# Moving the activation blocks and split weights of a 17,544-matmul chain by multiples of 64 bytes, and four raw weight buffers instead of five

## Chip, cores and metric

The kernel runs on one core of a Trainium2 chip. The metric is the device time in microseconds, the median of three runs.

## The reference, cut to what matters

A first block (rms norm, three groups of dilated attention and a state space model in parallel, gates, an output product, a SwiGLU with 2816 hidden features) is applied to a sequence x of 256 tokens with 1024 features. Two layers of a second block follow, each a SwiGLU, an attention mix and another SwiGLU, on x and on a context of 256 tokens, with modulation vectors silu(c) @ w_mod + b_mod. All is float32. The products with weight matrices are what matters here:

```python
def swiglu(xn, w_ffn_in, w_ffn_out):
    gate, up = jnp.split(xn @ w_ffn_in, 2, axis=-1)
    return (jax.nn.silu(gate) * up) @ w_ffn_out
```

## The kernel before

**Products.** Activations stand feature-major: a block is 128 features (partitions) by 256 tokens, 1,024 bytes a partition. A product works through weight slabs of 128 x 1024 numbers (4,096 bytes a partition): eight blocks k of 128 x 128 weights, one for each block of activations. Both factors are split into two float32r parts, a high one and the rest, and each block takes three matmuls of 256 columns (`mm3_k`, lines 128 to 130): high weights on high activations, high weights on low activations, low weights on high activations. Each of the three has a weight load of its own in front. A slab on one stream (x or the context c) is so 24 matmuls.

**Weights.** `load_raw` (line 102) loads a slab on SP's queue into a buffer of the pool `raw` (five). `split_w` makes the high part on ScalarE (line 109, tile `wh`) and the rest on VectorE (line 110, tile `wl`), in pools of five buffers each. A `wh` or `wl` buffer comes free when TensorE has used it for all streams; a raw buffer when both splits have read it. `run` prepares a slab up to two units of work ahead, and in the products with two streams the second one follows the first by a distance. The framework's planner orders each engine's queue and picks the buffers from its own estimate of when they come free, so a raw buffer is not always the one used longest ago.

**Background.** The modulation vectors are made on VectorE: a piece loads a slab of w_mod into a raw buffer and multiplies it with silu(c) of one or two streams (line 938, tile `junk`), adding along the row. 144 pieces are spread between the units of the products by `weave`: 16 in the SwiGLU of the first block, up to 40 in each of the first three SwiGLUs of the second block. A SwiGLU is 68 units (22 gate, 22 up, 24 down); pieces stand between the seventh unit and the ninth from the end.

**Activations.** `new_act` gives a stream the tiles `ah` and `al` (high and low part), eight blocks each, one block directly behind the other. The hidden features of a SwiGLU are tiles of one block each (`hh`, `hl`), from pools of 14. The last part of the state space model is `ynh`, `ynl`; the attention's output in the first block `aoh`, `aol`.

**Places.** The compiled program lays the tiles of a pool one behind the other in a partition's memory. The start bytes of the operands of lines 128 to 130, and what is left over after division by 128:

| tiles | first start byte | pitch, bytes | remainder mod 128 |
|---|---|---|---|
| wh (5 buffers), and each 512-byte block in them | 42,176 | 4,096 | 64 |
| wl (5 buffers) | 62,656 | 4,096 | 64 |
| ah, al of x | 106,560 and 114,752 | 1,024 a block | 64 |
| ah, al of c | 131,136 and 139,328 | 1,024 a block | 64 |
| hh, hl (all) | 147,520 and 161,856 | 1,024 | 64 |
| ynh, ynl | 197,504 and 201,600 | 1,024 a block | 0 |
| aoh, aol | 152,096 and 156,192 | 1,024 a block | 32 |

One unit of the first block, the step size of the state space model (`w_dt`), has 32 weight columns a block instead of 128, so its weight load reads 128 bytes a partition instead of 512; its activations are `ah`, `al` of x.

Of the kernel before, what the change touches and what calls it, by code (L numbers as in the profile page):

```python
# [44 lines left out]
class Unit:  # L45
    """n weight slabs of src from index `at`, and what is done with them for each stream."""
# [5 lines left out]
def weave(units, steps, start=0, stop=0):  # L52
    """The steps spread evenly between the units, from the unit start on, up to stop units before the end."""
# [10 lines left out]
class Builder:  # L64
    def __init__(self, ctx, tc, A):
# [3 lines left out]
        self.raw_p = self.pool(ctx, "raw", 5)  # L69
# [8 lines left out]
        self.X, self.ACT, self.acc, self.bg, self.deferred = {}, {}, {}, [], []  # L78

# [19 lines left out]
    # ---------------------------------------------------------------- weights  # L99
# [5 lines left out]
    def split_w(self, raw, f):  # L105
        nc = self.nc
        h = self.w_p.tile([128, 1024], F32R, name="wh")
        lo = self.w_p.tile([128, 1024], F32R, name="wl")
        nc.scalar.copy(h[:, :f], raw[:, :f])  # L109
        nc.vector.tensor_tensor(lo[:, :f], raw[:, :f], h[:, :f].bitcast(F32), op=ALU.subtract)  # L110
        return h, lo
# [5 lines left out]
    def mm3(self, out, w, acts, m=128, first=True, last=True):  # L117
        """out[m, t] += sum over k of w[k, m] * act[k, t], each factor as the sum of two float32r parts."""
# [17 lines left out]
    def stream(self, s, src):  # L136
        """A stream of tokens, feature-major: the residual and what goes into the next product."""
# [5 lines left out]
    def new_act(self, s, n=KB):  # L143
        h = self.act_p[s].tile([128, n, T], F32R, name="ah" + s, tag="ah")
        lo = self.act_p[s].tile([128, n, T], F32R, name="al" + s, tag="al")
        return h, lo
# [4 lines left out]
    def lin(self, src, i, acts, evac, m=128, streams=None):  # L151
        """A unit of work: the product of slab i of src with acts(stream), feature-major, to evac(stream, psum)."""
        return Unit(src, i, 1, None, streams, (acts, m, evac))

    def later(self, f, key=None):
        """f is issued behind the next unit of work: TensorE does not wait for what f needs."""
        self.deferred.append((key, f))

    def step(self):
        """What was put off so far."""  # L160
# [4 lines left out]
    def flush(self, keys=None):  # L165
        """What was put off, or only what belongs to the keys, is issued now."""
# [8 lines left out]
    def run(self, items, streams, done=None, ko=0, ahead=2):  # L175
        """Units in order; the second stream follows the first at a distance, so that the end of one hides
        behind the other. The first ko units go k-outer in the last stream, while its activations are being made.
        Items that are no units are just called."""
# [76 lines left out]
    def background(self, n=1):  # L255
        """The next n pieces of the modulation vectors."""
# [6 lines left out]
    # ------------------------------------------------------------------ norms  # L263
# [10 lines left out]
    def rstd_cols(self, p, n, scale, eps, newton=False):  # L274
        """1 / sqrt(p * scale + eps) of [128, n] sums of squares, a token to a partition."""
# [6 lines left out]
        if newton:  # L282
            # one step on 1 / sqrt(v): r * (1.5 - 0.5 * v * r * r)
# [7 lines left out]
    def sums(self, key):  # L291
        """The sums of squares with a token to a partition."""
# [6 lines left out]
    def on_all(self, r):  # L299
        """A column for each 128 tokens -> the same row on every partition, in PSUM."""  # L300
# [6 lines left out]
    def rstd_all(self, key, width, eps=1e-6):  # L307
        """1 / sqrt(mean of squares + eps) of each token, on every partition (in PSUM)."""
        return self.on_all(self.rstd_cols(self.sums(key), 2, 1.0 / width, eps))

    def norm(self, s, src, scale, shift, h, lo, r):
        """(src * scale) * r + shift of each block, as float32r parts."""
# [10 lines left out]
    def norm_stream(self, s, scale, shift, final=None):  # L323
        """The normed and modulated stream, for the next products; behind the next two units of work.
        final: the gain of a norm of the residual itself that comes first (the sums of its squares: s + "f")."""
# [37 lines left out]
    # -------------------------------------------------------------------- ffn  # L363
    def ffn(self, wg, wu, wds, streams, gate, hid_p, steps, done, after=None):
# [28 lines left out]
        # what a product down needs is ready some units before it  # L393
# [1445 lines left out]
```

## Time and profile before

| | |
|---|---|
| runs | 2560.78, 2562.79, 2567.07 us; median 2562.79 us |
| profiled execution, span from the first to the last instruction | 2558.6 us |
| TensorE busy | 2486.2 us, 97% of the span |
| VectorE busy | 1656.2 us, 65% |
| ScalarE busy | 1082.6 us, 42% |
| mean granted clock of TensorE | 0.985 |

The profiled execution's own time is not listed apart from its span; the span is 4.2 us under the median of the runs. Matmuls overlap in the records (each is shown as some 0.28 us long), so the busy share of TensorE doesn't tell how fast it goes: the distance from one start to the next does.

### The profile page before, as it was taken

To read this page: it belongs to the slowest core of one execution; us is meant where nothing else is said; L and a number is where in the kernel's file an instruction comes from. 1 tells how busy PE (TensorE), PEld (TensorE's weight loads), DVE (VectorE), ACT (ScalarE), POOL (GpSimd) and SP (SyncE) were. 2 spreads that over 40 slices of the span, in tenths; PEclk is the share of its full clock that TensorE was granted. 3 is DMA by queue.
4 is the path that set the end of the run, shared out by engine and by line. 5 is a ranking of instruction groups with operands and counts; after the bars stand their busy time and mean duration, and the time that the engine had idled before them with its cause. 6 is when DMAs were issued, how large, how long until landed. Compare 5 with 4: busy or idle time off the path is not lost.

```text
span 2558.6 us, 48101 instructions
## 1 busy us (share of the span) xinstructions
PE 2486.2 (97%) x19910; PEld 2359.6 (92%) x19910; DVE 1656.2 (65%) x3135; ACT 1082.6 (42%) x2057; POOL 15.7 (1%) x20
## 2 busy tenths in 40 slices
PE   6999999999999999999999999999999987999999
PEld 6999899999999999996599999999999987866999
DVE  4667787787766665768766666566454464667554
ACT  4557565535522322536743222243222243555443
POOL 0000000000000000000000000000000000000000
PEclk9999899999999999999999999999999998999999
DMA  7444455676444443331025444425455433332553
GB/s 225 148 155 160 133 165 188 209 246 202 153 160 159 161 154 120 122 113 59 1 71 167 157 158 158 143 98 165 149 167 163 135 92 80 105 95 81 173 181 124
DMA packets 117242, 364.28 MB, mean 142 GB/s; under 512 B 21050, under 2 KB 28730, under 8 KB 117024
## 3 DMA queue, kind: packets, MB, share of 16 engines
q1 hardware_dynamic: 114512, 355.73, 42.7%
q0 software_dynamic: 1008, 3.09, 1.0%
q8 instruction: 156, 2.56, 0.4%
q10 hardware_dynamic: 1504, 2.40, 0.3%
q14 instruction: 62, 0.51, 0.1%
HBM read 357.34 MB, written 3.82 MB: 141 GB/s over the span
## 4 chain that ended last, share of the span: by engine, by line
PE 59%; DMA 8%; DVE 5%; issue 2%; ACT 1%; DVEq 0%; ACTq 0%; SPq 0%
PE pm L128 17%; PE pm L129 16%; PE pm L130 16%; DMA wraw<-w_mod 7%; DVE junk L938 3%; DVE wl L110 2%; PE pt L1077 1%; DMA sin<-mla_sin 1%; PE pa L984 1%; PE pt L1008 1%; PE pa L1524 1%; PE pm L1276 1%; PE pm L1216 1%; PE pa L1292 0%; PE pm L1532 0%
## 5 line engine op out<-in xcount | busy, mean ns | idle before, releaser
L128 PE MATMUL pm<-ahx,wh 128*128 128x256 f32 x2936 | 841.7, 289 | 17.6 <-ACT q L483 8.0
L109 ACT CAST wh<-wraw 128x1024 fp32r<-128x1024 f32 (+4 forms) x535 | 539.9, 1012 | 707.1 <-PE pm L129 440.0
L129 PE MATMUL pm<-alx,wh 128*128 128x256 f32 x2936 | 834.9, 285 | 0.1
L130 PE MATMUL pm<-ahx,wl 128*128 128x256 f32 x2936 | 834.8, 285 | 0.0
L110 DVE TENSOR_TENSOR wl<-wraw,wh 128x1024 fp32r<-128x1024 f32 (+4 forms) x535 | 627.8, 1176 | 206.7 <-ACT wh L109 205.2
L128 PEld LDWEIGHTS pm<-ahx,wh 128*128 128x128 f32 x2936 | 558.3, 191 | 28.4 <-ACT q L483 8.2
L129 PEld LDWEIGHTS pm<-alx,wh 128*128 128x128 f32 x2936 | 560.5, 191 | 4.5 <-issue 2.7
L130 PEld LDWEIGHTS pm<-ahx,wl 128*128 128x128 f32 x2936 | 559.5, 191 | 2.7 <-issue 2.0
L128 PE MATMUL pm<-ahc,wh 128*128 128x256 f32 x1280 | 361.7, 284 | 4.4 <-ACT ahc L320 4.4
L130 PE MATMUL pm<-ahc,wl 128*128 128x256 f32 x1280 | 360.8, 282 | 0.0
L129 PE MATMUL pm<-alc,wh 128*128 128x256 f32 x1280 | 360.3, 282 | 0.0
L938 DVE SCALAR_TENSOR_TENSOR junk<-wraw,cactc 128x1024 f32<-128x1024 f32 x112 | 137.1, 1224 | 237.9 <-DMA wraw<-w_mod 237.9
L938 DVE SCALAR_TENSOR_TENSOR junk<-wraw,cactx 128x1024 f32<-128x1024 f32 x144 | 175.8, 1221 | 118.6 <-DMA wraw<-w_mod 117.6
L128 PE MATMUL pm<-hhx,wh 128*128 128x256 f32 x880 | 248.9, 283 | 0.0
L130 PE MATMUL pm<-hhx,wl 128*128 128x256 f32 x880 | 248.2, 282 | 0.0
L129 PE MATMUL pm<-hlx,wh 128*128 128x256 f32 x880 | 247.7, 281 | 0.0
L128 PEld LDWEIGHTS pm<-ahc,wh 128*128 128x128 f32 x1280 | 240.7, 189 | 6.8 <-ACT ahc L320 5.0
L130 PEld LDWEIGHTS pm<-ahc,wl 128*128 128x128 f32 x1280 | 241.5, 189 | 0.3
L129 PEld LDWEIGHTS pm<-alc,wh 128*128 128x128 f32 x1280 | 241.2, 189 | 0.6 <-DVE alc L321 0.2
L128 PEld LDWEIGHTS pm<-hhx,wh 128*128 128x128 f32 x880 | 165.9, 188 | 0.2 <-DVE xx L401 0.2
L129 PEld LDWEIGHTS pm<-hlx,wh 128*128 128x128 f32 x880 | 166.0, 189 | 0.0
L130 PEld LDWEIGHTS pm<-hhx,wl 128*128 128x128 f32 x880 | 165.6, 188 | 0.0
(465 smaller groups left out, 3339.2 us busy)
## 6 DMA issues: line engine op xcount, KB each, us to landing
wraw<-w_mod SPq DMA_DIRECT2D x144, 512.0 KB, 4.3
wraw<-f1g SPq DMA_DIRECT2D x44, 512.0 KB, 3.5
wraw<-f1u SPq DMA_DIRECT2D x44, 512.0 KB, 3.5
wraw<-f2g SPq DMA_DIRECT2D x44, 512.0 KB, 3.5
wraw<-f2u SPq DMA_DIRECT2D x44, 512.0 KB, 3.6
wraw<-f1d SPq DMA_DIRECT2D x32, 512.0 KB, 3.9
wraw<-f2d SPq DMA_DIRECT2D x32, 512.0 KB, 3.5
wraw<-w_xbc SPq DMA_DIRECT2D x24, 512.0 KB, 3.5
```

The costliest lines, as they stand in the source:

```text
L109: nc.scalar.copy(h[:, :f], raw[:, :f])
L110: nc.vector.tensor_tensor(lo[:, :f], raw[:, :f], h[:, :f].bitcast(F32), op=ALU.subtract)
L128: nc.tensor.matmul(out, h[:, c], ah, start=first, stop=False)
L129: nc.tensor.matmul(out, h[:, c], al, start=False, stop=False)
L130: nc.tensor.matmul(out, lo[:, c], ah, start=False, stop=last)
L938: nc.vector.scalar_tensor_tensor(junk, raw, 1.0, K.cact[s], op0=ALU.mult, op1=ALU.mult, accum_out=K.mcol[layer, s][:, j:j + 1])
L984: nc.tensor.matmul(self.p[:, c:c + nh], sq[self.rows, j * 128:(j + 1) * 128], self.sums, start=True, stop=True)
L1008: nc.tensor.matmul(r, self.sel[:, cs], self.r, start=True, stop=True)
L1077: nc.tensor.transpose(p[:, j * 128:(j + 1) * 128], b, K.ident)
L1216: nc.tensor.matmul(p[:, :nk], qa[s][rows, 2 * half + b, t * 128:(t + 1) * 128], ka[rows, k0:k0 + nk], start=True, stop=True)
L1276: nc.tensor.matmul(p[:, :nk], qb[s][rows, hd, t * 128:(t + 1) * 128], kb[rows, hd, k0:k0 + nk], start=True, stop=True)
L1524: nc.tensor.matmul(po[64 * e:64 * e + 64, :T], v[:, i, b * 128 + e * 64:b * 128 + e * 64 + 64], pts[i][:, e * 256:e * 256 + 256], start=i ...
```

## The change

The two parts of the activations get blocks of 272 numbers of which 256 are used, so a block starts 1,088 bytes behind the one before. The buffers of the split weights are 1,072 numbers long, and a slab stands 0, 64, 128 or 192 bytes behind the start of its buffer: the high part by the number of the split modulo 4, the low part by a quarter of that number modulo 4. Raw weights get four buffers. Comments and docstrings are dropped without a change in line numbers up to the constructor; one line is added there (`self.n_split`), and two in `split_w`.

```diff
-        self.raw_p = self.pool(ctx, "raw", 5)
+        self.raw_p = self.pool(ctx, "raw", 4)
...
+        self.n_split = 0
...
     def split_w(self, raw, f):
         nc = self.nc
-        h = self.w_p.tile([128, 1024], F32R, name="wh")
-        lo = self.w_p.tile([128, 1024], F32R, name="wl")
+        self.n_split += 1
+        place = lambda t, i: t[:, 16 * (i % 4):16 * (i % 4) + 1024]
+        h = place(self.w_p.tile([128, 1072], F32R, name="wh"), self.n_split)
+        lo = place(self.w_p.tile([128, 1072], F32R, name="wl"), self.n_split // 4)
...
     def new_act(self, s, n=KB):
-        h = self.act_p[s].tile([128, n, T], F32R, name="ah" + s, tag="ah")
-        lo = self.act_p[s].tile([128, n, T], F32R, name="al" + s, tag="al")
-        return h, lo
+        h = self.act_p[s].tile([128, n, T + 16], F32R, name="ah" + s, tag="ah")
+        lo = self.act_p[s].tile([128, n, T + 16], F32R, name="al" + s, tag="al")
+        return h[:, :, :T], lo[:, :, :T]
```

## Rows read from the trace of the kernel before

**Rows 1.** The page: span, busy time and instructions of each engine.
```profile
span 2558.6 us, 48101 instructions
...
PE 2486.2 (97%) x19910; PEld 2359.6 (92%) x19910; DVE 1656.2 (65%) x3135; ACT 1082.6 (42%) x2057; POOL 15.7 (1%) x20
```

**Rows 2.** Four SwiGLUs by stretch: span, busy us (instructions) of each engine, clock, DMA.
```profile
475.00:640.00 165.00, 164.71 (x1378) 163.98 (x1377) 128.25 (x197) 78.86 (x115) 0.00 (x0) 1.00 0.67 225
...
1345.00:1640.00 295.00, 294.73 (x2484) 294.52 (x2482) 189.28 (x323) 77.87 (x127) 0.00 (x0) 1.00 0.49 158
```

**Rows 3.** TensorE's groups by line: count, busy us, mean ns.
```profile
L128 PE MATMUL pm<-ahx,wh 128*128 128x256 f32 x2936 | 841.7, 289 | 17.6 <-ACT q L483 8.0 <-ACT ahx L320 6.2 <-ACT ahx L114 2.0
...
L128 PE MATMUL pm<-ahc,wh 128*128 128x256 f32 x1280 | 361.7, 284 | 4.4 <-ACT ahc L320 4.4
...
L128 PE MATMUL pm<-hhx,wh 128*128 128x256 f32 x880 | 248.9, 283 | 0.0
...
L128 PE MATMUL pm<-hhc,wh 128*128 128x256 f32 x528 | 148.7, 282 | 0.0
```

**Rows 4.** Timeline of TensorE, last SwiGLU, one stream: start us, length.
```profile
2500.02 0.28 PE L128 MATMUL pm<-hhx,wh 128*128 128x256 f32 x1
...
2504.34 0.28 PE L128 MATMUL pm<-ahx,wh 128*128 128x256 f32 x1
```

**Rows 5.** Timeline of TensorE, a SwiGLU with two streams.
```profile
1450.07 0.28 PE L128 MATMUL pm<-hhx,wh 128*128 128x256 f32 x1
...
1455.05 0.28 PE L128 MATMUL pm<-hhx,wh 128*128 128x256 f32 x1
```

**Rows 6.** Timeline of TensorE, three units with ynh, and an entry from aoh.
```profile
402.17 0.28 PE L128 MATMUL pm<-ynh,wh 128*128 128x256 f32 x1
...
404.64 0.28 PE L128 MATMUL pm<-ynh,wh 128*128 128x256 f32 x1
...
406.79 0.28 PE L130 MATMUL pm<-ynh,wl 128*128 128x256 f32 x1
...
410.19 0.28 PE L130 MATMUL pm<-ynh,wl 128*128 128x256 f32 x1
...
411.73 0.28 PE L128 MATMUL pm<-ynh,wh 128*128 128x256 f32 x1
...
412.20 0.28 PE L129 MATMUL pm<-ynl,wh 128*128 128x256 f32 x1
```

**Rows 7.** Timeline of TensorE, the unit with 32 weight columns.
```profile
110.64 0.28 PE L128 MATMUL pm<-ahx,wh 128*32 128x256 f32 x1
...
111.22 0.28 PE L130 MATMUL pm<-ahx,wl 128*32 128x256 f32 x1
...
112.92 0.28 PE L130 MATMUL pm<-ahx,wl 128*32 128x256 f32 x1
```

**Rows 8.** SP's loads by source, 1340 to 1660 us: count, ns min/median/max, first and last start.
```profile
L102 SPq DMA_DIRECT2D wraw<-w_mod x39: 327/328/328, 1345.6 to 1639.6; - x39
```

**Rows 9.** The chain of waits, 1403 to 1412 us: start, us, what.
```profile
1404.48 4.38 DMA wraw<-w_mod
```

**Rows 10.** SP's loads by source, 490 to 600 us; one semaphore step a load.
```profile
L102 SPq EVENT_SEMAPHORE  x54: 17/17/3548, 491.2 to 599.7; - x54
...
L102 SPq DMA_DIRECT2D wraw<-w_mod x13: 327/328/737, 493.4 to 574.9; - x13
```

**Rows 11.** VectorE's waits, 500 to 600 us: total, times, longest.
```profile
DVE junk L938 <- DMA wraw<-w_mod: 12.0, 12, 3.0
```

**Rows 12.** The page: splits and pieces by line: count, busy us, mean ns.
```profile
L109 ACT CAST wh<-wraw 128x1024 fp32r<-128x1024 f32 (+4 forms) x535 | 539.9, 1012 | 707.1 <-PE pm L129 440.0
...
L110 DVE TENSOR_TENSOR wl<-wraw,wh 128x1024 fp32r<-128x1024 f32 (+4 forms) x535 | 627.8, 1176 | 206.7 <-ACT wh L109 205.2
...
L938 DVE SCALAR_TENSOR_TENSOR junk<-wraw,cactc 128x1024 f32<-128x1024 f32 x112 | 137.1, 1224 | 237.9 <-DMA wraw<-w_mod 237.9
```

**Rows 13.** DMA issues by line: count, KB, median us to landing.
```profile
wraw<-w_f_g SPq DMA_DIRECT2D x22, 512.0 KB, 4.5
```

## The prediction

> **What bounds the kernel now.** Begin with the share of busy time. TensorE is busy for 97% of the span [rows 1], so the time goes there, but matmuls overlap in the records, and a busy TensorE may still go slower than it could. Next come the stretches: in the SwiGLUs the granted clock is 1.00, the 2.4 GHz level, and PE and PEld are busy throughout [rows 2]. So the question is the distance between two starts there, and that only the timeline tells, row by row.
>
> In the last SwiGLU, 36 matmuls go by between the two rows shown, in 4.32 us: 120.0 ns each [rows 4]. In a SwiGLU with two streams 42 matmuls take 4.98 us: 118.6 ns [rows 5]. The unit with `ynh` is the one to stop at: 30 matmuls in 3.40 us, 113.3 ns [rows 6]. All have 256 columns, the same clock, the same weight buffers. What differs by the table of places is where the moving block begins: at remainder 64 modulo 128, as the weights do, or at 0. The second hint is the unit with 32 weight columns. Its blocks are the very ones at remainder 64, and it goes at 113.3 ns (15 matmuls in 1.70 us) [rows 7]. A weight load that reads a quarter of the bytes frees the matmul beside it. So the two reads of a matmul and a weight load disturb each other by 5.3 to 6.7 ns a matmul, and the places of both seem to decide it.
>
> There is a caution in the same rows. Another `ynh` unit, with the same remainders, stays at 117.6 ns (21 matmuls in 2.47 us, 402.17 to 404.64) [rows 6]. And on entering a `ynh` unit from `aoh`, the first four distances take 0.47 us, 117.5 ns each, before it runs at 113.3 [rows 6]; the short unit likewise starts with five at 116 (0.58 us) [rows 7]. The short distance is reached after some matmuls, and not always.
>
> **The change part by part: the places.** A block of 1,088 bytes is 8.5 times 128, so the eight blocks of a product lie at remainder 64, 0, 64, 0 and so on; within a block k all three matmuls keep it. A buffer of 4,288 bytes is 33.5 times 128, and with the shift by 64 bytes a split the remainder of a slab is 0 or 64, each for about half of the slabs. For `ah` and `al` half of the matmuls of each unit then run with equal remainders and half with unequal ones, whatever the slab; for `hh` and `hl` the same holds over the slabs.
>
> The matmuls that are touched: 2936 + 1280 + 880 + 528 = 5,624 of each of the three lines, 16,872 in all [rows 3]. The lower bound of the gain is nothing (118.7 ns stays). If every unequal matmul went at 113.3 and every equal one stayed at 118.7, the mean would be 116.0 and the gain 16,872 x 2.7 ns = 46 us. But the remainder now changes every three matmuls, and the nearest row for that is the entry into `ynh`, where the first four still take 117.5. Were none of a run of three better than that, the gain would be 0.5 x 1.2 ns x 16,872 = 10 us. I take a mean of 116.8, nearer to the halves, as on leaving a quick stretch the long distances should come late too: 1.9 ns x 16,872 = 32 us. The products outside this count (`ynh`, `aoh`, the short ranks, the token-major ones) are a few per cent of it and can go either way; they are costed at nothing.
>
> The Trainium skill speaks against this change: "TensorE: Matmul & The Clock Gate", in its step by step of what happens when a matmul is issued (Part 2), gives TensorE two independent SBUF read ports, one for the streaming operand and one for the weight load, and says that loading the next weights takes no read bandwidth from the running matmul. By that rule this term is zero. The trace doesn't agree: with the same moving tile, 113.3 ns stand beside the short load and 118.6 to 120.0 beside the full one [rows 4, 5, 7].
>
> **What VectorE gives back.** In the three two-stream SwiGLUs TensorE's gain can't be taken whole. A piece of background goes round on its own: the load takes 4.38 us [rows 9], the two `junk` operations 2 x 1.22 [rows 12], and the queue behind waits. 39 pieces were loaded in 294.0 us, 38 distances of 7.74 us [rows 8]. TensorE gives a piece 54/40 units of two times 24 matmuls, 64.8 matmuls: 7.69 us at 118.7 and 7.57 at 116.8. So now VectorE falls behind by 0.05 x 40 = 2 us in such a SwiGLU and then by 0.17 x 40 = 7 us. The five `wh` buffers hide a few microseconds of it; the bounds are 0 and 7 for each of the three, and I take 2, together 6 us lost.
>
> **Four raw buffers.** In the two-stream SwiGLUs a raw buffer is not short: 1.35 slabs and a piece come every 7.7 us, and each needs its buffer for a load and its reading, 4.4 + 2.4 us, so 2.35 x 6.8 / 7.7 = 2.1 buffers would do. The tight place is the first block's SwiGLU: 54 loads between 491.2 and 599.7 us [rows 10], one every 2.0 us, so five buffers are held 10.2 us each, four would have 8.2. The need is 4.5 [rows 13] + 1.01 + 1.18 [rows 12], 6.7 us. It fits, with 1.5 us to spare. Below, the cost is nothing; above, each of the 13 pieces there waits a load longer, 13 x 2.0 = 26 us of VectorE's time, in a stretch where it idles 12 us on such loads already [rows 11] and is busy 128 of 165 us [rows 2]. Nearer to the fit, I take 4 us. What waits behind a late `junk` is the next `wl` on VectorE and with it TensorE's next slab.
>
> The splits and the evictions do the same work on rows of the same length, one block at a time; their costs don't change.
>
> **Sum**, against the profiled span: 2558.6 - 32 + 6 + 4 = 2536.6. The span lies 4.2 us under the median of the runs; with that, 2540.8, say 2540 us, 0.9% less.
>
> **The rivals.** *All unequal pairs are quick, and starts on 128 bytes are quick for each operand by itself.* Then three quarters of the matmuls go at 113.3 and a quarter at 118.7, a mean of 114.7: 4.0 x 16,872 = 68 us; VectorE then lags by (7.74 - 7.43) x 40 = 12 us a SwiGLU, some 6 of them felt, 18 in all. 2562.8 - 68 + 18 + 4 = 2517 us. For it: the `ynh` unit is the one with its block at 0. Against it: the unit at 117.6.
>
> *The places don't matter.* The quick `ynh` unit is then an accident of timing, as the slow one at the same places suggests, and a weight load is slow or quick by its length alone [rows 6, 7]. 2562.8 us, and with the raw buffers' 4 us 2567. Against it: the quick `ynh` unit holds 113.3 ns over 30 matmuls [rows 6], which no full weight load at equal remainders does in [rows 4, 5]. A change that never lets the short distance come about ends here as well. The rule of the Trainium skill cited above, in "TensorE: Matmul & The Clock Gate", Part 2, gives this case too.
>
> *Changing remainders cost* (slower). Each change upsets both streams, as the entry into `ynh` shows: four distances of 117.5 against 113.3 are 17 ns a change. With eight changes in 24 matmuls that is 5.6 ns a matmul on top of the 116.0 of the halves, 121.6 for the 12,648 matmuls on `ah` and `al`: +2.9 x 12,648 = 37 us, less 2.7 x 4,224 = 11 us on the hidden features: 2589 us. It decides from 8 ns a change on (2.7 x 3). Against it: on entry no distance was longer on the mean than the 118.7 of before, so leaving a quick stretch should pay back a part.
>
> *The raw ring binds* (slower): 26 us in the first block's SwiGLU and half a microsecond more for each of some 118 pieces elsewhere, 59 us, against the gain of 32: about 2616 us. It needs a hold above 8.2 us.
>
> **How the numbers follow.** A measurement of this kernel tells 0.3% (8 us) from no change. The forecast, between 2522 and 2555, has 0.45; the better rival, 2500 to 2522, 0.18; no effect, 2555 to 2570, 0.20; changes that cost 0.10; the ring 0.07. Faster is 0.63, same 0.20, slower 0.17. Leaving out the two slower rivals and the tail of the better one, the range is 2500 to 2570; the likeliest case's own is 2522 to 2555.
>
> **What would show it.** Right: in the last SwiGLU the distances alternate in runs of three and average 116 to 118 instead of 120; units with hidden features are of two kinds, near 113 and near 119; the first block's SwiGLU stays without stalls. The forecast is wrong if the mean distance stays at 118 or more, if it falls under 115, or if TensorE waits for `wl` in the SwiGLUs with pieces.

## The result, and the profile after

The changed kernel takes 2581.68 us (2579.45 to 2587.97, three runs) against 2562.79 us: a ratio of 1.008 with a 95% interval of 1.0051 to 1.0108. It is 0.8% slower, where the prediction said 2540 us and a range of 2500 to 2570. The profiled execution has a span of 2579.6 us, 21.0 us more than before. In the changed kernel the three matmul lines are 131 to 133 (128 to 130 before), the splits 112 and 113, and the other helpers stand three lines further down. Three executions among the runs below, of 6,589, 6,071 and (the kernel before) 11,451 us, are left out of medians and ratios.

The page of the changed kernel, its first part:

```profile
span 2579.6 us, 48110 instructions
PE 2479.4 (96%) x19910; PEld 2345.5 (91%) x19910; DVE 1657.1 (64%) x3135; ACT 1079.4 (42%) x2057; POOL 15.3 (1%) x20
```

TensorE is busy for 7 us less than before [rows 1] in a span that is 21 us longer, so the loss is idle time: 72.4 us of the span before, 100.2 us now. First, though, the pace, as the prediction asked. The timeline of TensorE in the changed kernel, the last SwiGLU (39 matmuls between the two rows) and then a SwiGLU with two streams (21 between the first two rows, 42 between the last two):

```profile
2499.91 0.28 PE L131 MATMUL pm<-ahx,wh 128*128 128x256 f32 x1
...
2504.49 0.28 PE L131 MATMUL pm<-ahx,wh 128*128 128x256 f32 x1
```

```profile
1450.13 0.28 PE L131 MATMUL pm<-hhx,wh 128*128 128x256 f32 x1
...
1452.61 0.28 PE L131 MATMUL pm<-hhc,wh 128*128 128x256 f32 x1
...
1453.30 0.28 PE L131 MATMUL pm<-hhc,wh 128*128 128x256 f32 x1
...
1458.06 0.28 PE L131 MATMUL pm<-hhc,wh 128*128 128x256 f32 x1
```

On `ahx`, whose remainder changes every three matmuls, the distance is 4.58 us / 39 = 117.4 ns, against 120.0 [rows 4]. Part of that is no gain of the places: in the run with only the raw buffers changed (`raw4` below), whose places are those of before, the last SwiGLU goes at 118.7 ns. On hidden features the remainder of the moving block stays for a whole slab. Two units stand in the rows: 2.48 us / 21 = 118.1 ns and 4.76 us / 42 = 113.3 ns, against 118.6 [rows 5]. They are no two kinds: in the last SwiGLU, 2410 to 2545 us, the units of 24 matmuls on hidden features have means from 113.3 to 119.7 ns, those on `ahx` from 116.4 to 119.7, and all together 117.7. So the places do act, by about 1 ns on the mean, and the quick pace over a whole unit comes only on some units whose moving blocks keep their remainder.

Next, TensorE's waits over the whole execution of the changed kernel (total us, times, longest):

```profile
PE pm L131 <- ACT ahx L323: 31.1, 6, 25.9
PE pm L131 <- ACT ahx L117: 12.8, 3, 10.7
...
PE pt L298 <- DVE acc L275: 8.6, 7, 2.8
```

The same view of the kernel before:

```profile
PE pt L295 <- DVE acc L272: 22.0, 5, 15.4
...
PE pm L128 <- ACT q L483: 8.0, 1, 8.0
...
PE pm L128 <- ACT ahx L320: 6.2, 6, 1.1
...
PE pm L128 <- ACT ahx L114: 2.0, 2, 1.0
```

Two waits have grown: one of 25.9 us on the activations of x at the start of the second attention mix, one of 10.7 us at the start of the program. Both stand where the kernel before waits as well, for something else: 15.4 us on `acc` at the start of the second attention mix, 8.0 us on `q` at the start. What they cost is the difference, and that is read by stretch. The traces hold the same 19,910 instructions of TensorE in nearly the same order, so the start of the n-th in one can be set against the start of the n-th in the other. Windows of the changed kernel that hold the same matmuls as those of the kernel before underneath (span, busy us and instructions of PE, PEld, DVE, ACT, POOL, then the granted clock), first the SwiGLUs that have pieces, then the start, the end of the first attention mix with its output product, and the start of the second attention mix:

```profile
478.38:645.09 166.71, 164.11 (x1377) 162.46 (x1376) 130.37 (x199) 79.47 (x115) 0.00 (x0) 1.00 0.69 224
706.14:1008.06 301.92, 298.55 (x2512) 296.28 (x2511) 189.98 (x324) 77.32 (x129) 0.00 (x0) 1.00 0.50 157
1358.28:1656.67 298.39, 294.39 (x2484) 293.00 (x2483) 188.26 (x321) 76.73 (x127) 0.00 (x0) 1.00 0.50 159
1737.55:2072.91 335.36, 333.14 (x2825) 332.39 (x2824) 173.84 (x292) 90.83 (x151) 0.00 (x0) 1.00 0.48 153
0.00:64.44 64.44, 41.53 (x266) 37.69 (x267) 27.89 (x49) 27.01 (x45) 3.77 (x10) 0.89 0.72 199
1248.16:1323.48 75.32, 70.72 (x441) 56.67 (x441) 43.56 (x100) 41.27 (x82) 0.00 (x0) 0.89 0.09 28
2097.53:2205.07 107.54, 75.67 (x601) 73.80 (x602) 51.16 (x128) 42.29 (x104) 1.38 (x2) 0.84 0.36 82
```

And of the kernel before; the first and the third SwiGLU are the windows of [rows 2]:

```profile
700.09:1000.05 299.96, 298.90 (x2512) 298.04 (x2510) 188.12 (x320) 78.64 (x129) 0.00 (x0) 1.00 0.48 156
1720.11:2055.10 334.99, 334.99 (x2825) 334.99 (x2824) 173.76 (x291) 91.49 (x151) 0.00 (x0) 1.00 0.47 152
0.00:60.08 60.08, 40.44 (x266) 37.10 (x267) 28.02 (x49) 27.44 (x45) 3.77 (x10) 0.94 0.80 223
1240.11:1310.04 69.93, 65.36 (x442) 53.49 (x441) 43.58 (x100) 41.06 (x82) 0.00 (x0) 0.95 0.09 31
2080.16:2180.02 99.86, 78.06 (x601) 76.55 (x602) 51.45 (x128) 42.28 (x104) 1.38 (x2) 0.86 0.38 86
```

In the four SwiGLUs with pieces TensorE now idles 2.6, 3.4, 4.0 and 2.2 us, 12.2 together against 1.6 before; what it waits for there is by its waits mostly VectorE's products with its results (`g`, `xx`, `xc`), and `wl` for 0.5 us once. At the end of the first attention mix the same matmuls take 5.4 us longer with the same idle time (4.6 us in both windows): the granted clock is 0.89 instead of 0.95. Over the whole span the mean granted clock is 0.980 against 0.985, and 2579.6 x 0.020 = 52 us against 2558.6 x 0.015 = 38 us of full-speed time were not granted. But much of that fell on idle time: TensorE was busy for 54 us of the lower level before and for 64 us now, and half of the difference, 5 us, is what the clock cost by itself. What the lower level means for one instruction stands in the chain of waits, for the same group of eight matmuls in the first attention mix. Of the kernel before, at a granted clock of 1.00 (1256.00 to 1257.50 us):

```profile
1256.18 1.09 PE pa L1292 x8
```

Of the changed kernel, at 0.50, the 1.2 GHz level (1264.90 to 1267.00 us):

```profile
1264.94 2.00 PE pa L1295 x8
```

The account of the 21.0 us, from matmul to matmul: the changed kernel falls behind by 4.3 us in the first 60 us of the kernel before, by 5.4 at the end of the first attention mix and by 7.7 at the start of the second. From 475 to 700, 700 to 1000, 1345 to 1720 and 1720 to 2055 us, the SwiGLUs with pieces and their ends, it loses another 2.8, 2.0, 4.2 and 0.4 us in spite of the quicker pace. It wins 3.0 us in the last SwiGLU and 2.8 us elsewhere. The pace by itself is worth some 19 us: 1,584 matmuls of the last SwiGLU by 2.4 ns (2 us of this are the slower pace that the kernel before happened to have there) and the other 15,288 by about 1.0 ns (118.6 to 117.6, from the windows of the kernels without pieces below). All of it, and more, goes into pauses and clock. This is one trace of each kernel; what of it the change brings about is for the experiments to tell.

### The profile page after: what moved, and what is told of

Same layout as the page of the kernel before. It is cut to its first block, busy times and chain, and to the rows that moved or that the text cites. A ratio compares the mean times of both kernels' runs of the same rounds, so it can differ in the third digit from the quotient of the medians.

```text
span 2579.6 us, 48110 instructions
## 1 busy us (share of the span) xinstructions
PE 2479.4 (96%) x19910; PEld 2345.5 (91%) x19910; DVE 1657.1 (64%) x3135; ACT 1079.4 (42%) x2057; POOL 15.3 (1%) x20
## 4 chain that ended last, share of the span: by engine, by line
PE 40%; DMA 18%; DVE 11%; issue 4%; ACT 2%; DVEq 0%; ACTq 0%; SPq 0%
DMA wraw<-w_mod 16%; PE pm L131 10%; PE pm L132 10%; PE pm L133 10%; DVE junk L941 5%; DVE wl L113 4%; PE pt L1080 1%; DMA sin<-mla_sin 1%; PE pa L987 1%; PE pm L1279 1%; PE pt L1011 1%; PE pa L1527 1%; PE pm L1219 1%; ACT wh L112 1%; PE pa L1295 1%
## 5 line engine op out<-in xcount | busy, mean ns | idle before, releaser
L131 PE MATMUL pm<-ahx,wh 128*128 128x256 f32 x2936 | 836.8, 287 | 48.7 <-ACT ahx L323 31.1
L941 DVE SCALAR_TENSOR_TENSOR junk<-wraw,cactx 128x1024 f32<-128x1024 f32 x144 | 175.7, 1220 | 118.2 <-DMA wraw<-w_mod 117.2
L117 ACT CAST hhc<-g 128x256 fp32r<-128x256 f32 x66 | 26.8, 406 | 400.0 <-DVE g L380 400.0
```

What stands on the lines that cost most here:

```text
L117: self.nc.scalar.copy(h, src)
L131: nc.tensor.matmul(out, h[:, c], ah, start=first, stop=False)
L941: nc.vector.scalar_tensor_tensor(junk, raw, 1.0, K.cact[s], op0=ALU.mult, op1=ALU.mult, accum_out=K.mcol[layer, s][:, j:j + 1])
```

## The experiments

Each median stands beside runs of the kernel before on the same chip; those medians lie between 2561.3 and 2565.4 us. The ratios compare all executions, not the two medians, so the two can differ by a few microseconds. Where a trace is set against that of the kernel before matmul by matmul, the text says "by matching", and the times of a stretch are those of the kernel before.

**The two halves of the change: the raw buffers alone, the places alone.**

```diff
-        self.raw_p = self.pool(ctx, "raw", 5)
+        self.raw_p = self.pool(ctx, "raw", 4)
```

> The kernel before with four raw weight buffers and nothing else. Theory A (the ring): the places gained some 18 us (16,900 matmuls, 118.7 to 117.7 ns from start to start) and the smaller ring cost the rest, 37 us: 2590 to 2605 us, with TensorE's stalls in the SwiGLUs with pieces and at the start. Theory B (the pieces' round): the ring costs next to nothing, and a quicker TensorE only meets the VectorE round of 7.7 us a piece sooner: 2557 to 2571 us, the order of matmuls at 118.7 ns as before.

Measured: 2584.11 us, ratio 1.0062 (1.0038 to 1.0086): 16 us by the ratio, 20 by the medians. The four raw buffers alone cost about as much as the whole change. TensorE's waits with them:

```profile
PE pm L128 <- ACT ahx L320: 31.2, 6, 26.0
PE pm L128 <- ACT ahx L114: 11.1, 3, 9.1
```

These are the two grown waits of the changed kernel, without any of its places. What the second one stands behind is seen in the waits of the first 60 us with four buffers:

```profile
ACT wh L109 <- DMA wraw<-w_q: 12.8, 2, 12.0
DVE alx L115 <- ACT ahx L114: 11.3, 1, 11.3
```

A split of w_q stands in ScalarE's queue and waits 12.0 us for its load; the cast of the activations is queued behind it. With five buffers ScalarE waits as well, one slab later, with the cast already done:

```profile
ACT wh L109 <- DMA wraw<-w_k: 10.6, 2, 10.4
```

So the start loses 5.7 us by matching and not 9.1, and the start of the second attention mix 8.0. In the first block's SwiGLU, where the prediction looked for the cost, TensorE is busy for 164.09 of 165 us (475 to 640), against 164.71 [rows 2]. In the four SwiGLUs with pieces together it idles 6.7 us (matched windows) against 1.6, without any change of places: so the ring costs something there, too.

The places alone: the changed kernel with five raw buffers. To make room, `e` has six buffers instead of eight and the pool `tmp` nine instead of ten.

> The changed kernel with five raw buffers; to make room, the softmax tiles e have 6 buffers in place of 8 and the temporary tiles 9 in place of 10. Theory A (the ring): the places' gain shows, 2540 to 2552 us, with the first block's SwiGLU and the first two-stream SwiGLU shorter than in the changed kernel. Theory B (the pieces' round): no better than 2570 us, since TensorE's gain is given back in the SwiGLUs with pieces in any case; only the last SwiGLU is shorter than before by 3 to 5 us. Both: start to start 117.4 to 118 ns.

Measured: 2555.49 us, ratio 0.9965 (0.995 to 0.998). The places gain 8.5 us where the prediction had 32 less 6. The medians of the two halves add up to 12 us of loss, those of the whole change to 19; with three runs of the change that difference is not clear of noise.

**The kinds of difference.** Only the blocks of the activations 1,088 bytes apart (`new_act` as in the change, `e` with seven buffers), so that the remainder changes from block to block, always against the same weights:

> The kernel before with the activation blocks 1,088 bytes apart and nothing moved in the weights, five raw buffers; the tiles e have 7 buffers in place of 8. If a change of the remainder every three matmuls keeps the quick state from being reached: 117.3 to 118.5 ns on ah, 118.7 to 120 on hh as before, 2550 to 2565 us. If half of the matmuls were quick: 116 ns on ah and 2530 to 2545 us.

Measured: 2551.73 us, ratio 0.9948 (0.9929 to 0.9967). Its profile has a granted clock of 1.00 between 230 and 290 us, where before and after have 0.83; 9 us come from there by matching, so the time says little about the pace. The distances do: from 1720 to 2050 us 2790 of TensorE's instructions take 330.00 us, 118.3 ns each, and in the five SwiGLUs `ah` goes at 118.2 to 118.3 ns, `hh` at 118.6 to 118.7. That is the first expectation. Alternation against weights that stay put gains about 0.4 ns, no matmuls at 113.3 over a whole unit.

Weights and activations at different remainders that never change, by an unused tile between their pools:

```diff
         self.w_p = self.pool(ctx, "wsplit", 5)
+        self.pad = self.pool(ctx, "pad", 1).tile([128, 16], F32, name="pad")
```

> The kernel before with one unused tile of 64 bytes behind the split weights, so that every activation and hidden block lies at remainder 0 modulo 128 while the weights stay at 64: unequal remainders everywhere, and no change from block to block. If a constant unequal remainder is what the quick state needs: 113 to 114 ns from start to start on ah and hh, the last SwiGLU 193 to 183 us, and 2490 to 2530 us in all, held up in the three SwiGLUs with 40 pieces by the pieces' round (40 x 7.7 us). If the places are no cause (timing alone): 118 to 120 ns and 2555 to 2571 us.

Measured: 2543.97 us, ratio 0.9915 (0.9891 to 0.994). With 48 numbers in the unused tile, 192 bytes:

> The kernel before with an unused tile of 192 bytes behind the split weights: remainder 0 modulo 128 for the activations as with 64 bytes, but the other distance modulo 256 between moving block and weights (64 in place of 192). If only the remainder modulo 128 counts: 113.3 or 117.8 ns and 2535 to 2550 us as with 64 bytes. If the distance modulo 256 counts as well, as hidden features in the changed kernel suggest (113.3 ns at 192, near 117 at 64): 116.5 to 118 ns throughout and 2550 to 2562 us.

Measured: 2555.63 us, ratio 0.997 (0.9953 to 0.9987), near the upper of the two expectations. By windows 1720 to 2050 us it made 2804 matmuls in 330.00 us, 117.7 ns each. The remainders modulo 128 are those of the run with 64 bytes, so modulo 128 is not the whole rule, and a difference that holds still is not enough for the quick pace.

The run with 64 bytes shows both paces, and what lies between. The timeline of TensorE with 64 bytes:

```profile
1848.92 0.28 PE L129 MATMUL pm<-hhx,wh 128*128 128x256 f32 x1
...
1851.52 0.28 PE L131 MATMUL pm<-hhx,wl 128*128 128x256 f32 x1
1853.01 0.36 PE L129 MATMUL pm<-ahc,wh 128*128 128x256 f32 x1 [1.21 <-DVE xc L402]
1853.20 0.28 PE L130 MATMUL pm<-alc,wh 128*128 128x256 f32 x1
...
1855.91 0.28 PE L129 MATMUL pm<-hhx,wh 128*128 128x256 f32 x1
```

Up to 1851.52 us 23 distances take 2.60 us, 113 ns each; then TensorE waits 1.21 us; from 1853.20 on 23 take 2.71 us, 117.8 each, and it stays so to 2060 us (1,755 distances); between 2400 and 2530 us 1106 matmuls take 130.00 us, 117.5 each. Nothing in the layout has changed. With a constant difference there are two paces, and a pause can turn one into the other. Not each does: in the same stretch 920 distances at 113.3 ns end in a pause of 1.12 us, and the pace stays. It goes the other way, too. With 64 bytes and own buffers for the pieces (below), two windows before and behind a pause of 1.93 us, with 117.8 ns from start to start in the first and 113.4 in the second:

```profile
1549.00:1572.00 23.00, 22.36 (x190) 22.16 (x189) 16.26 (x29) 6.79 (x11) 0.00 (x0) 1.00 0.86 269
1574.00:1638.00 64.00, 64.00 (x567) 64.00 (x567) 29.24 (x47) 18.25 (x28) 0.00 (x0) 1.00 0.35 115
```

**The pieces' round.** Pieces get two raw buffers of their own for the time of a SwiGLU:

```diff
-    def load_raw(self, src):
-        t = self.raw_p.tile([128, 1024], F32, name="wraw")
+    def load_raw(self, src, own=None):
+        t = own.tile([128, 1024], F32, name="mraw") if own else self.raw_p.tile([128, 1024], F32, name="wraw")
...
+        K.mraw = K.pool(fctx, "mraw", 2)
```

On the kernel before:

> The kernel before, with two buffers of their own for the slabs of w_mod while a SwiGLU runs; places and the five raw buffers as before. If the pieces' round on VectorE (load, two junk, next load) only just keeps up, VectorE's waits for w_mod shrink from 356 us to under 150 us; TensorE, at 118.7 ns, was not held up by it but for a few us: 2548 to 2565 us. If the round is not what holds VectorE, its waits for w_mod stay above 300 us.

Measured: 2573.67 us, ratio 1.0043 (1.0027 to 1.006). The time missed. VectorE's wait on w_mod did go (47.6 us on the own buffers, the kernel before has 355.5), but pieces now stand early in VectorE's queue, among the last operations ahead of a SwiGLU and ahead of its first splits. By matching it loses 6.9 us at the entry into the first block's SwiGLU (440 to 475 us), where TensorE is busy for 49.04 of 60 us (440 to 500) at a clock of 0.89, the kernel before for 55.46 at 0.94; and 4.5 and 5.0 us from 640 to 700 and from 1310 to 1345. On the changed kernel:

> The changed kernel (four raw buffers, moved places) with two buffers of their own for w_mod while a SwiGLU runs. If the small ring harms by sharing its buffers with the pieces in the SwiGLUs, 2555 to 2568 us: the first two-stream SwiGLU no longer loses 3 us to the kernel before and the second no longer 5, and what stays is the start (4 us) and the beginning of the last attention mix (9 us). If the pieces are no cause, 2575 to 2585 us and the same losses in both SwiGLUs.

Measured: 2577.84 us, ratio 1.0058 (1.0038 to 1.0079). Missed as well. Against own buffers on the kernel before, the change now costs 4 us instead of 19.

With the 64 bytes:

> The kernel before with the unused tile of 64 bytes behind the split weights and two buffers of their own for w_mod while a SwiGLU runs. If the pieces' round is what kept the constant shift from paying in the SwiGLUs with two streams, they get shorter by 10 to 15 us each where the quick state holds (113.3 ns): 2505 to 2530 us. If it isn't, 2538 to 2550 us as with the shift alone.

Measured: 2533.29 us, ratio 0.9885 (0.986 to 0.9909), the best of all and ahead of both kernels. Own buffers cost 11 us on their own, yet with them the 64 bytes gain 40 us, and without them 20. A window of the first two-stream SwiGLU, with 64 bytes only:

```profile
700.00:1000.00 300.00, 291.27 (x2483) 287.64 (x2481) 187.45 (x319) 75.76 (x126) 0.00 (x0) 1.00 0.49 155
```

With 64 bytes and own buffers:

```profile
700.00:1000.00 300.00, 300.00 (x2649) 300.00 (x2648) 142.79 (x222) 83.53 (x136) 0.00 (x0) 1.00 0.36 113
```

300 us / 2649 = 113.3 ns without a pause, against 8.7 us of idle time and both paces (113.3 and 117.8). So in this SwiGLU the shared buffers hold TensorE back. In the second one it idles 9.7 of 295 us (1345 to 1640) with own buffers, too. The trace is of the quickest of the five executions, 2522.47 us.

Own buffers only in the first SwiGLU of each layer, with 64 bytes:

> The kernel before with 64 bytes between weights and activations throughout and two own buffers for w_mod, opened only for the first SwiGLU of each layer. With own buffers in all four SwiGLUs it was 2533, with none 2544. Theory: in the first SwiGLUs the pieces' round held TensorE back, and opening the buffers for the block ahead and for the second SwiGLU cost more than it gave (7 and 6 us at their starts): 2518 to 2530. Rival: own buffers pay in every SwiGLU alike, so half of the gain is lost: 2536 to 2542.

Measured: 2560.44 us, ratio 0.9998 (0.9984 to 1.0012). Both theories missed. Its trace has the slow pace from 800 to 1050 and from 1350 to 1550 us. Its largest loss by matching is one place, though: between 1640 and 1720 us, where the second SwiGLU ends and the next layer's first one opens its own buffers, it falls 21 us behind the kernel before, at a clock of 0.80 from 1700 to 1720. That opening the buffers costs at the entries was part of the theory; that it takes the whole gain was not.

**Where four raw buffers cost.** At the start of the second attention mix two things meet. The chain of waits of the changed kernel:

```profile
2102.83 3.64 DMA wraw<-cd_cq
...
2111.12 31.93 DMA sin<-mla_sin
2143.07 0.35 DVE xc L1054
2143.42 0.40 DVE y L319
2143.84 0.52 ACT ahx L323
```

With one buffer less the first slab of cd_cq lands late, and in the order that the planner writes for VectorE the operation that needs mla_sin now stands ahead of `y`, the normalisation of x. The load of mla_sin takes 31.93 us beside the broadcast of a table, so the activations of x wait for a table that they don't use. The kernel before has the two the other way round, by VectorE's timeline; the same load then holds a split and `acc`, the sums of squares, and that is its wait of 15.4 us:

```profile
2105.46 0.86 DVE L316 SCALAR_TENSOR_TENSOR y<-xx,mcol1x,pt 128x256 f32<-128x256 f32 x2
...
2117.85 0.35 DVE L1050 TENSOR_SCALAR xc<-cos,cols 96x256 f32<-96x256 f32 x1 [8.52 <-DMA cos<-mla_cos]
```

Its chain of waits:

```profile
2094.62 31.14 DMA sin<-mla_sin
...
2127.85 0.34 DVE acc L272
```

One more raw buffer for two loads, the fifth of the program and the first of cd_cq:

```diff
-    def load_raw(self, src):
-        t = self.raw_p.tile([128, 1024], F32, name="wraw")
+    def load_raw(self, src, one=False):
+        self.n_load += 1
+        one = one or self.n_load == 5
+        t = (self.one_p if one else self.raw_p).tile([128, 1024], F32, name="wone" if one else "wraw")
```

> The kernel before with four raw buffers and one more buffer that only two loads use: the fifth load of the program and the first of the six loads of cd_cq. Four raw buffers alone gave 2584 against 2564. Theory: most of that comes from two late slabs (the fifth load, for which ScalarE and then TensorE wait some 10 us at the start, and the first slab of cd_cq, behind which TensorE's wait on ahx grew from some 4 to 26 us): then 10 to 16 us come back, 2566 to 2574, and that wait is under 8 us again. Rival: four buffers cost a little with every piece of background: 2578 or more.

Measured: 2570.99 us, ratio 1.004 (1.0025 to 1.0055). Met; by the ratios the gain on four raw buffers alone is 6 us, barely clear of noise, by the medians 13. Its wait on the activations of x:

```profile
PE pm L131 <- ACT ahx L323: 6.3, 6, 1.1
```

The two tables still take 23.6 and 31.1 us here; only the order has changed back, and with it the wait on `acc` (15.1 us). By matching, the start of the second attention mix loses 0.3 us instead of 8.0, and the start of the program is no longer behind. So the order is the cause there, not the slow load by itself.

The loads of mla_cos and mla_sin on SP's queue instead of ScalarE's, on the changed kernel:

```diff
-    nc.scalar.dma_start(cos[r96], A["mla_cos"])
-    nc.scalar.dma_start(sin[r96], A["mla_sin"])
+    nc.sync.dma_start(cos[r96], A["mla_cos"])
+    nc.sync.dma_start(sin[r96], A["mla_sin"])
```

> The changed kernel with the two loads of mla_cos and mla_sin on SP's queue instead of ScalarE's; TensorE's order is the same, and on VectorE the two operations that need them stand behind the normalisation of x instead of ahead of it. Theory: at the start of the second attention mix TensorE waits 25.9 us on ahx because VectorE waits there for a 32 us transfer of mla_sin ahead of that normalisation: the wait falls under 8 us and the time to 2560 to 2574. Rival: the slabs of cd_cq are slow at that place anyway, and the wait only moves to them: 2576 to 2584.

Measured: 2570.64 us, ratio 1.0034 (1.0017 to 1.005). Met, and the wait on `ahx` is 6.5 us in six. The edit does two things at once: the order changes, and the loads, now issued 4 us ahead of the broadcast, take 2.9 and 2.7 us. On the kernel before:

> The kernel before with the same move of the two loads. There the normalisation of x stood ahead of the operations that wait for mla_sin already. Theory: little to win, 2555 to 2563, and changed and unchanged kernel then stand 8 to 14 us apart instead of 19. Rival: the transfer holds the unchanged kernel as much as the changed one, and both win the same, 10 us or more: 2553 or less.

Measured: 2562.67 us, ratio 0.9988 (0.9971 to 1.0005). Met: the edit gives nothing where the order was right, though the loads are as quick there (2.4 and 2.1 us). By the times the edit gives back 11 of the changed kernel's 19 us. By matching it is 6.1 us at the place itself, which loses 1.6 us instead of 7.7, and another 5.1 at the end of the first attention mix, ahead of it, where this trace has 6.8 us of the lower clock and the changed kernel's 17.1. So the place is a third of the loss, and of the stretch with the clock it isn't shown that the change brings it about: the waits ahead of it are the same.

Both edits on four raw buffers:

> Four raw buffers, one more for the two loads, and mla_cos and mla_sin on SP's queue. If the two edits mend different halves of the ring's cost, the time is that of the kernel before, 2558 to 2566. If both mend the same place (the start of the second attention mix), it stays at 2567 to 2574, and the rest lies with the background pieces or the other order in the first attention mix.

Measured: 2570.75 us, ratio 1.0042 (1.0023 to 1.0062). Not the first expectation: they do not add up. By matching, the two mended places lose 0.6 and 1.3 us, and the largest piece of the 10.2 us that remain in its trace is again the end of the first attention mix, 4.0 us. Without a change of remainder, four raw buffers and 64 bytes:

> Four raw buffers and 64 bytes between weights and activations throughout: the change without its alternation. Theory: the alternation every three matmuls took the gain from the places; without it some 18 us are gained on the 2582 to 2584 of four buffers, 2560 to 2570, in spite of the ring. Rival: with four buffers every gain is eaten by late slabs: 2576 or more.

Measured: 2559.89 us, ratio 1.0004 (0.9977 to 1.003), 24 us less than four buffers alone. At the lower end of what was expected: the constant difference pays with four buffers as well. With both edits in addition:

> The same with the extra buffer for two loads and the two loads on SP's queue. Theory: both costs are gone and the constant difference gains what it gained with five buffers: 2538 to 2552, ahead of both kernels. Rival: the pieces' round holds four buffers harder than five: 2555 or more.

Measured: 2550.36 us, ratio 0.995 (0.9926 to 0.9974). Met.

**Without the pieces.** The loads of w_mod and the `junk` operations are left out:

```diff
-            raw = K.load_raw(K.A[f"w_mod{layer}"][j])
             for s in who:
-                junk = pool.tile([128, D], F32, name="junk")
-                nc.vector.scalar_tensor_tensor(junk, raw, 1.0, K.cact[s], op0=ALU.mult, op1=ALU.mult,
-                                               accum_out=K.mcol[layer, s][:, j:j + 1])
+                nc.vector.memset(K.mcol[layer, s][:, j:j + 1], 0.1)
```

> The kernel before without its 144 pieces of background: neither the loads of w_mod nor the junk operations, the modulation vectors are set to a constant. It is the measure for the next two. By the trace TensorE hardly waits for the pieces there, so 2550 to 2562; more than 12 us less would mean that they slow the matmuls by other ways than waits.

Measured: 2552.81 us, ratio 0.9949 (0.993 to 0.9968), 12.6 us less, at the edge of the two expectations. In its profile, of a quick execution (2548.71 us), most of that lies in one stretch with another clock, shown at the end of this section. The pace in the two-stream SwiGLUs is not quicker for it: 118.7 ns from start to start from 700 to 1000 us, as with the pieces. The mean clocks of its executions have a median of 0.9865 against 0.985, some 4 us, so for the median the rest stays open.

> Four raw buffers with the two edits, and no pieces (modulation vectors set to a constant). If the remaining cost of the ring lies in the pieces: within 3 us of the kernel before without pieces. If it lies elsewhere (the other order in the first attention mix, slabs at the ends of products): 7 to 11 us above that.

Measured: 2561.41 us, ratio 0.9984 (0.9968 to 1.0), 8.6 us over the one before it. By this difference the remaining cost of four buffers does not lie in the pieces; the caution below says why that isn't shown.

> The changed kernel without the pieces (modulation vectors set to a constant). If the pieces took the gain of the places and half of the ring's cost: 2 to 10 us below the kernel before without pieces. If the places give nothing even where nothing waits: 10 us or more above it, as with the pieces.

Measured: 2558.22 us, ratio 0.9972 (0.9957 to 0.9987), 5.4 us over the kernel before without pieces, between the two expectations. The change costs 5 us without pieces and 19 with them, so the pieces take about 13 us, known to some 6. The idle time counted above in the SwiGLUs, 12.2 against 1.6 us, is of that size. The changed kernel without pieces, by windows:

```profile
700.00:1000.00 300.00, 300.00 (x2551) 300.00 (x2550) 110.35 (x161) 82.41 (x131) 0.00 (x0) 1.00 0.29 92
1345.00:1640.00 295.00, 295.00 (x2507) 295.00 (x2507) 109.43 (x159) 82.43 (x132) 0.00 (x0) 1.00 0.30 95
```

No pause is left, and the pace is 117.6 and 117.7 ns: that is what the places of the change are worth in two-stream SwiGLUs. The first window of the kernel before without pieces gives 300.00 us for 2530, 118.6 ns.

A caution on the 8.6 us. The stretch from 230 to 290 us in the kernel before without pieces:

```profile
230.00:290.00 60.00, 59.47 (x476) 54.39 (x476) 53.46 (x101) 42.24 (x89) 0.00 (x0) 1.00 0.51 161
```

And in the four-buffer kernel without pieces:

```profile
230.00:290.00 60.00, 59.34 (x398) 51.95 (x397) 45.34 (x85) 32.45 (x65) 0.00 (x0) 0.83 0.41 130
```

60 x 0.17 = 10 us of the 13 us between these two profiles lie in one stretch with a lower clock, and outside it they differ by 2.9. The kernel before has 0.83 there with five buffers and with pieces, so the stretch is not the ring's. It is similar over all runs with pieces: the median of the mean granted clock is 0.986 in the runs of before and 0.983 in those of four buffers with both edits, 2561.3 x 0.014 = 36 us and 2570.75 x 0.017 = 44 us not granted, a difference of 8 us where 9 remain. That goes together and is no proof of a cost: what isn't granted while TensorE idles costs nothing, and one run of the kernel before has a mean clock of 0.936 and took 2570.16 us.

## Why the prediction was wrong, step by step

**The places** were right in that the starts matter, and too large: 32 us were predicted (a mean of 116.8 ns), about 19 came (117.7 in the last SwiGLU, 117.6 in the others without pieces). The step that failed is "I take a mean of 116.8, nearer to the halves". It averaged over matmuls as if half of each unit could run at 113.3, and the row of the entry into `ynh` [rows 6], which the prediction had as its lower reading (117.5, 10 us), described the whole of `ah` and `al`. The quick pace was seen over whole units only where the difference holds, as in some slabs of hidden features and with 64 bytes between the pools, and not always there. The mean of 116 to 118 ns in the last SwiGLU came as predicted. Runs of three with alternating distance did not appear, nor two kinds of units with hidden features, and the prediction's picture of the places was too simple for them: high and low weights are shifted by two different counts, so in about half of the slabs they stand at different remainders, and the relation to the moving block then changes within a block as well. That this is why the units' means spread from 113 to 120 ns fits, and was not tested.

**Changing remainders cost** is refuted as a rival: no unit was slower than the 118 to 120 ns of before, and the mean is lower. Single groups of three do reach 122 ns. **The places don't matter** is refuted by 113.3 ns over 300 us with 64 bytes. The Trainium skill gives that rival in "TensorE: Matmul & The Clock Gate", Part 2 (two independent read ports, a weight load that takes nothing from the running matmul); the runs do not bear it out, 113.3 against 117.7 ns for the same instructions with 64 and 192 bytes between the pools.

**What VectorE gives back** was predicted as 6 us, 2 for each two-stream SwiGLU. TensorE's idle time in the SwiGLUs with pieces grew by 10.6 us: 2.3, 2.3, 3.7 and 2.2. Not all of it is VectorE's round: with four raw buffers alone it grew by 5.1. The round of 7.74 us was right (39 distances of 7.78 us in the changed kernel); that five `wh` buffers hide it was not, and the wait is not for `wl`, the prediction's sign, but for VectorE's products with TensorE's results.

**Four raw buffers** is the step that turned the sign. 4 us were predicted, in the first block's SwiGLU ("It fits, with 1.5 us to spare"). They cost 16 to 20 us, and little of it there. The prediction reckoned buffers by rate: need against hold. In that SwiGLU the rate was fine. What counted most were single loads at places where work begins: the fifth slab of the program, behind which ScalarE's cast of the activations waits (TensorE 10.7 us, where it waited 8.0 before; 4.3 us by matching), and the first slab of cd_cq, behind which the order of VectorE's queue is another, so that a 32 us load stands ahead of TensorE's input (25.9 us, where it waited 15.4 before; 7.7 us by matching). Both waits go with a buffer for these two loads. The rival "the raw ring binds" had the sign and most of the place wrong: it put the cost on every piece, and the SwiGLUs with pieces have 5 us of it.

**What was missing altogether** is the clock. The prediction read a clock of 1.00 in the SwiGLUs and costed a wait at its length. At 1.2 GHz the work takes nearly twice as long (1.09 against 2.00 us for the same eight matmuls). By the two means 13 us more were not granted; by TensorE's busy time 5 of the 21 us go with the clock. The Trainium skill has this in "TensorE: Matmul & The Clock Gate", Part 1, on oscillation: half of the time at the lower level is the price. The traces agree: 60 us at a mean of 0.83, 20 of them at the lower level, hold 398 of TensorE's instructions, and at 1.00 they hold 476; the 78 between them are 10 us of full speed (60 / 476 = 126 ns each).

**Open.** With both places mended, four buffers still cost some 9 us. 4 of them lie by matching at the end of the first attention mix, where only the clock differs, the rest in small pieces; whether four buffers make the lower clock more frequent there, or these traces happened to have it, was not tried. Nor is it settled why the same layout has two paces, nor which pause turns one into the other.

## What to carry to other kernels

Before a ring gets a buffer less, look at the loads that start a phase, not only at the mean rate: one late slab there can go with another order of a queue and cost more than the steady stretches. A new wait in a list is not its cost: look at what the old program waited for at the same place, best by setting the same instruction's start in both traces side by side. A gain in pace is paid out only as far as the engine with the next longer round allows, so measure it once with that engine's load taken out. And a pause can cost time after it as well: the lower clock level stands around the 25.9 us wait of the changed kernel for 34 us.

## What the runs showed of the hardware that was not expected

A float32r matmul of 256 columns, each with a full weight load, ran at two steady paces with one and the same layout: 113.3 ns for 300 us on end, or 117.8, with the change from one to the other at a pause of 1.21 us, and back at one of 1.93. Before, with equal remainders, two steady paces were there as well, 118.6 and 120.0 [rows 4, 5], and the last SwiGLU has either, by the run. 64 bytes between weights and activations gave the quick one in some stretches, 192 bytes nearly never (2804 matmuls in 330.00 us), though modulo 128 the two are equal. With the remainder of the moving block changing every three matmuls, the mean stayed at 117.6 to 117.8 ns in every SwiGLU when the weights moved, too, and at 118.2 to 118.3 on `ah` when they did not.
